# Copying the scan's products out of PSUM on ScalarE and masking them in SBUF on GpSimd

## The chip, the cores and the metric

The kernel runs on one core of a Trainium2 chip. Such a core has five engines with queues of their own: TensorE (PE in the profile, and PEld for its weight loads), VectorE (DVE), ScalarE (ACT), GpSimd (POOL) and SyncE (SP), which here only issues transfers. Matrix products land in PSUM; the other operands live in SBUF. GpSimd has no operation on PSUM in this kernel. An engine carries out its queue in order, and an instruction at the head of a queue that waits for another engine holds what is behind it.

The metric is the device time of one execution in microseconds (us), taken as the median of several runs.

## The reference, cut to what matters

One layer of an encoder: a half-step feed-forward network, a mixing layer, a second half-step feed-forward network, on 1024 tokens of 1024 features in float32. The mixing layer has eight attention heads and eight heads of a recurrent scan, which runs in both directions. The scan's step is

```python
def _rwkv7_step(state, inp):
    r, w, k, v, kk, kka = inp
    sa = jnp.einsum('dbhvk,dbhk->dbhv', state, kk)
    state = state * w[..., None, :] - sa[..., :, None] * kka[..., None, :] + v[..., :, None] * k[..., None, :]
    y = jnp.einsum('dbhvk,dbhk->dbhv', state, r)
    return state, y
```

`d` is the direction (2), `h` the head (8), and the state of each is 64 x 64. 1024 such steps follow one another.

## The kernel before, in words

The scan is not stepped token by token. The 1024 tokens are cut into 16 chunks of `C` = 64, and two chunks (`BLK` = 2) make a block, so there are eight blocks. Inside a chunk the steps are solved as a triangular system, from products of the chunk's own vectors; only the 64 x 64 state goes from chunk to chunk. Four methods do the work for a block `n`:

- `prep` (line 783) loads the inputs for both directions `d`, scales them by the running decay, and forms the products inside each chunk. For each chunk `i` it fills two PSUM banks, one for each parity `par` of the head (`lp`, line 830): four head pairs side by side, 128 rows by 128 columns each. The rows are two halves of 64 tokens: the half `half(par)` holds the products with the vector called `kka` in the reference, the other half those with `k`. The columns are two halves as well: 0 to 63 with `kk`, 64 to 127 with `r`. A token may only see earlier ones, so each 64 x 64 quadrant has to be triangular: without its diagonal for `kk`, with it for `r`. On line 832 VectorE multiplies each bank by a table of zeros and ones (`tri`) and writes it to the tile `lm` in SBUF. The three PSUM banks of tag `pp` are shared by `lp` and by the transposes `bp` (line 838), which ScalarE copies out on line 840. At the end (line 846) four transfers on SP's queue store the diagonal 32 x 32 blocks of the quadrant `kka` by `kk` in DRAM.
- `solve` (line 850) loads them again as `X`, and VectorE inverts all of them at once in 31 steps of two small operations each (lines 866 and 868) that wait for one another. GpSimd's queue then stores the inverse (lines 872 and 873).
- `merge` (line 875) loads the inverse over GpSimd's queue (lines 883 and 886) and joins the 32 x 32 inverses to 64 x 64 by products (lines 894 and 900). It reads the part of `lm` that lies above the diagonal blocks, in the same quadrant.
- `chain` (line 918) goes through the two chunks. On line 928 it first overwrites the quadrant `kka` by `kk` of `lm`, which is no longer needed, with other factors. For each chunk there are then the products `xu`, `st` and `y` (lines 937 to 952), ScalarE's copies between them (lines 944 and 954), VectorE's update of the state `sv` (line 968), and loads of values `uv` and `sv` on GpSimd's queue (line 908).

Blocks 0 and 1 are prepared among the last projections of the layer's input (lines 1269 and 1270). Then the loop over the blocks calls, for each `n`, `merge(n)`, `chain(n)`, and `upto(n + 3)`, which prepares and solves block `n + 3` (lines 1285 to 1299), so that up to three blocks are prepared ahead; `lm` has a buffer for each of them. Beside this, PE multiplies the attended values by their part of the output weights (`project_attended`, line 1066).

The framework's planner, which takes the order of the code as priority and goes by modelled costs, fixes the order of the instructions on each engine when the program is built, and places the waits between engines. A change to some instructions can therefore reorder their neighbours. Waits follow from the tiles' parts that are written and read.

The constants come in `mix_constants` (line 1146) and are made on the host in `_tables` (line 1394).

Of the kernel before, what the change touches and what calls it, by code (L numbers as in the profile page):

```python
# [13 lines left out]
OP = mybir.AluOpType  # L14
# [12 lines left out]
C, NC_, BLK = 64, 16, 2  # L27
# [4 lines left out]
def _ap(src, off, pat):  # L32
    return bass.AP(tensor=src.tensor, offset=src.offset + off, ap=pat)
# [130 lines left out]
class _Kernel:  # L164
# [618 lines left out]
    def prep(self, n, p, psum, big):  # L783

        nc, V, A, T = self.nc, self.nc.vector, self.nc.scalar, self.nc.tensor
        flat = lambda z: z.rearrange("p a t -> p (a t)")
        chunks = lambda z: z.rearrange("p a (i t) -> p a i t", i=BLK)
        ls = slice(n * TB, (n + 1) * TB)
        lm = big.tile([128, 2, 2, BLK, 4, 128], F32, name="lm", tag="lm")
        gc = big.tile([128, 2, 4, BLK], F32, name="gc", tag="gc")  # L790
        blk = dict(lm=lm, pr=[], bt=[], gc=gc)
        for d in range(2):
            b = n if d == 0 else NC_ // BLK - 1 - n
            ts = slice(b * TB, (b + 1) * TB)
            th = {}
            for nm in "wa":
                th[nm] = p.tile([128, 4, TB], F32, name="th_" + nm, tag="th_" + nm, bufs=2)
                self.load(th[nm], self.lr_d[nm][d][:, :, ls].rearrange("a p t -> p a t"))
            x3 = p.tile([128, 3, 4, TB], F32, name="in3", tag="in3", bufs=1)
            self.load(x3.rearrange("p j a t -> p (j a) t"), self.rk_d[:, :, ts].rearrange("a p t -> p a t"))  # L800
            x = {nm: x3[:, j, :, ::-1] if d else x3[:, j] for j, nm in enumerate(("r", "k", "kk"))}
            cum = th["w"]
            e1 = self.e1
            e4 = e1.rearrange("p (a i) t -> p a i t", i=BLK)
            A.activation(e4[:, :, :, 1:C + 1], chunks(cum), AF.Exp)
            A.activation(flat(cum), flat(cum), AF.Exp, scale=-1.0)
            ei = chunks(cum)
            V.tensor_copy(gc[:, d], e4[:, :, :, C])
            pt = big.tile([128, 4, BLK, 128], F32, name="pr", tag=f"pr{d}")
            V.tensor_tensor(pt[:, :, :, 0:C], chunks(x["kk"]), e4[:, :, :, 0:C], op=OP.mult)  # L810
            V.tensor_tensor(pt[:, :, :, C:], chunks(x["r"]), e4[:, :, :, 1:C + 1], op=OP.mult)
            bk = p.tile([128, 4, BLK, 192], F32, name="bk", tag="bk", bufs=2)
            bb = bk[:, :, :, 0:C]
            V.scalar_tensor_tensor(bb, chunks(th["a"]), 1.0, chunks(x["kk"]), op0=OP.add, op1=OP.mult)
            V.scalar_tensor_tensor(bb, bb, 0.5, ei, op0=OP.mult, op1=OP.mult)
            A.copy(bk[64:, :, :, 2 * C:], bk[64:, :, :, 0:C])
            kd = th["a"]
            for pr in range(4):
                A.activation(kd[:, pr, :], kd[:, pr, :], AF.Identity, scale=self.kah[:, pr:pr + 1],
                             bias=self.ka1[:, pr:pr + 1])  # L820
            V.tensor_tensor(kd, kd, x["k"], op=OP.mult)
            V.tensor_tensor(bk[:, :, :, C:2 * C], chunks(kd), ei, op=OP.mult)
            self.nc.sync.dma_start(self.kd_d[d][:, :, ls].rearrange("a p t -> p a t"), kd)
            bt = big.tile([128, BLK, 2, 4, 64], F32, name="bt", tag=f"bt{d}")
            both = [(slice(o, o + 64), o) for o in (0, 64)]
            for i in range(BLK):
                ps = [psum.tile([128, 4, 128], F32, name="lp", tag="pp") for par in range(2)]
                for pr in range(4):
                    for par, (hs, ko) in enumerate(both):
                        T.matmul(ps[par][:, pr, :], bk[hs, pr, i, ko:ko + 128], pt[hs, pr, i, :], start=True, stop=True)  # L830
                for par in range(2):
                    V.tensor_tensor(lm[:, par, d, i], ps[par], self.tri[:, None, :].to_broadcast([128, 4, 128]),
                                    op=OP.mult)
            pb = [psum.tile([128, BLK, 4, 64], F32, name="bp", tag="pp") for par in range(2)]
            for i in range(BLK):
                for pr in range(4):
                    for par, (hs, ko) in enumerate(both):
                        T.transpose(pb[par][:, i, pr, :], bk[hs, pr, i, ko:ko + 128], self.ident[hs, hs])
            for par in range(2):
                A.copy(bt[:, :, par], pb[par])  # L840
            for k, v in (("pr", pt), ("bt", bt)):
                blk[k].append(v)
        for par in range(2):
            for k in range(2):
                r0 = par * 64 + k * 32
                self.nc.sync.dma_start(_ap(self.x_d[n % 4], (k * 2 + par) * 16 * 1024, [[32, 32], [1024, 16], [1, 32]]),
                                  lm[r0:r0 + 32, par, :, :, :, k * 32:k * 32 + 32].rearrange("p d i a t -> p (d i a) t"))
        return blk
# [296 lines left out]

    def mix_constants(self, p):
        io = self.io
        for nm in ("ones2", "tri", "cen"):
            t = p.tile([128, 128], F32, name="k_" + nm)
            self.load(t, io["k_" + nm])  # L1150
            setattr(self, nm, t)
# [242 lines left out]
def _tables():  # L1394

    e = -np.arange(0, HD, 2, dtype=np.float32) / np.float32(HD)
    inv = np.power(10000.0, e.astype(np.float64)).astype(np.float32)
    ang = (np.arange(S, dtype=np.float32)[:, None] * inv[None, :]).astype(np.float64)
    c, s = np.cos(ang).astype(np.float32), np.sin(ang).astype(np.float32)
    i, j = np.arange(128)[:, None], np.arange(640)[None, :]  # L1400
    dist = np.abs(j - 256 - i)
    n = (dist <= 64).astype(np.int64) + ((dist <= 256) & (dist % 4 == 0))
    bias12 = np.where(n > 0, np.log(np.maximum(n, 1)), NEG).astype(np.float32)
    blk = np.arange(128) // 64
    same = blk[:, None] == blk[None, :]
    a = np.arange(64)
    lo, di = (a[:, None] < a[None, :]), (a[:, None] <= a[None, :])
    tri = np.tile(np.concatenate([lo, di], 1), (2, 1)).astype(np.float32)
    return {"k_rope": np.concatenate([c, c, -s, s], 1), "k_ones2": same.astype(np.float32), "k_tri": tri,
            "k_cen": (np.eye(128) - same / 64).astype(np.float32),  # L1410
            "k_bias12": bias12}

# [23 lines left out]
```

## Time and profile before

| | us |
|---|---|
| runs | 2351.04, 2352.01, 2360.32 |
| median | 2352.01 |
| profiled execution | 2359.91 |
| its span, first to last instruction | 2357.9 |
| mean granted TensorE clock | 0.956 |

The span is 2.0 us shorter than the profiled execution's time, and that execution lies near the slowest of the three runs. In the profile, "L832" is line 832 of the kernel. A group of instructions reads: line, engine, operation, output `<-` inputs by the program's names, shapes, count, then busy time in us and the mean duration in ns, then the engine's idle time just before them and what ended it. A row of the waits reads: who waited, for whom, total us, times, longest. In a timeline a row begins with its start and its duration in us. The scan's blocks are prepared from 1216 to 1503 us of the span, and its chunks run from 1312 to 1577 us; the feed-forward networks lie before and after, and take most of the span.

### The profile page before, as it was taken

Reading aid. Unit: us, or ns where it says so; the run is one execution under the profiler, and the core shown is the slowest. Engines: PE = TensorE matmul, PEld = TensorE weight load, DVE = VectorE, ACT = ScalarE, POOL = GpSimd, SP = SyncE. Lnnn points to the kernel's source line nnn. Section 1 sums busy time; section 2 is a strip of 40 time slices with the busy share of each in tenths; the row PEclk is TensorE's granted clock in tenths of the full one; section 3 lists DMA queues with packets and bytes.
Section 4 is the critical chain, followed back from the end, with each engine's and each line's share of the span. In section 5 each row is a group of like instructions: output and inputs, shape, how many; then the busy total and the mean of one; then the engine's idle time right before and its main releaser. Section 6 shows DMA issues by size and latency. Waiting matters only on the chain. (4 is left out here: it accounts for less than half of the span.)

```text
span 2357.9 us, 39484 instructions
## 1 busy us (share of the span) xinstructions
PE 2216.0 (94%) x14532; PEld 1788.8 (76%) x14532; DVE 1782.4 (76%) x2957; ACT 1035.0 (44%) x1958; POOL 609.7 (26%) x732
## 2 busy tenths in 40 slices
PE   6999999999999998999996899989699999999997
PEld 4788888878877676787775777766578888887886
DVE  8899999865676244766658778737899999986565
ACT  4332223354577412666554646445443323235453
POOL 6244444410000010111202242332334444441000
PEclk8999999999999998999997799989899999999999
DMA  5254544485662513323268877577434454547665
GB/s 157 98 171 154 177 143 170 166 262 193 207 217 85 200 45 120 99 79 81 68 167 201 212 187 197 140 233 250 156 108 168 167 174 143 174 156 258 193 191 180
DMA packets 359380, 386.04 MB, mean 164 GB/s; under 512 B 74258, under 2 KB 265618, under 8 KB 359188
## 3 DMA queue, kind: packets, MB, share of 16 engines
q1 hardware_dynamic: 308512, 276.43, 38.8%
q0 software_dynamic: 30320, 94.44, 11.2%
q10 hardware_dynamic: 20356, 12.66, 1.9%
q8 instruction: 114, 1.87, 0.3%
q14 instruction: 78, 0.64, 0.1%
HBM read 257.53 MB, written 125.89 MB: 163 GB/s over the span
## 5 line engine op out<-in xcount | busy, mean ns | idle before, releaser
L186 ACT ACTIVATE wh<-raw 128x512 fp32r<-128x512 f32 (+1 forms) x273 | 168.1, 626 | 267.4 <-PE gu L81 92.9
L81 PE MATMUL gu<-xh,wh 128*128 128x512 f32 x704 | 277.1, 394 | 1.1 <-ACT xh L186 1.1
L187 DVE TENSOR_TENSOR wl<-raw,wh 128x512 fp32r<-128x512 f32 (+1 forms) x273 | 273.8, 1006 | 4.4 <-ACT wh L186 3.2
L81 PE MATMUL gu<-xl,wh 128*128 128x512 f32 x704 | 276.1, 392 | 0.0
L81 PE MATMUL gu<-xh,wl 128*128 128x512 f32 x704 | 275.7, 392 | 0.0
L415 PE MATMUL pd<-gl,gwh 128*128 128x512 f32 x616 | 241.4, 392 | 3.0 <-DVE gl L187 3.0
L415 PE MATMUL pd<-gh,gwl 128*128 128x512 f32 x616 | 240.7, 391 | 0.0
L415 PE MATMUL pd<-gh,gwh 128*128 128x512 f32 x616 | 240.1, 391 | 0.4 <-DVE row L86 0.4
L86 DVE TENSOR_TENSOR row<-gu,row 128x512 f32<-128x512 f32 x308 | 206.4, 682 | 25.0 <-PE gu L81 24.6
L187 DVE TENSOR_TENSOR gwl<-graw,gwh 128x512 fp32r<-128x512 f32 (+1 forms) x176 | 116.9, 667 | 128.6 <-ACT gwh L186 126.5
L116 POOL DMA_DIRECT2D d_hid<-row x154 | 84.7, 551 | 473.3 <-DVE row L114 450.9
L186 ACT ACTIVATE gwh<-graw 128x512 fp32r<-128x512 f32 (+1 forms) x176 | 101.3, 576 | 189.9 <-PE pd L415 160.0
L81 PEld LDWEIGHTS gu<-xh,wh 128*128 128x128 f32 x704 | 133.4, 190 | 30.2 <-ACT xh L186 2.8
L81 PEld LDWEIGHTS gu<-xl,wh 128*128 128x128 f32 x704 | 133.3, 189 | 27.7
L81 PEld LDWEIGHTS gu<-xh,wl 128*128 128x128 f32 x704 | 133.1, 189 | 27.4
L415 PEld LDWEIGHTS pd<-gl,gwh 128*128 128x128 f32 x616 | 116.1, 188 | 28.2 <-DVE gl L187 4.3
L415 PEld LDWEIGHTS pd<-gh,gwh 128*128 128x128 f32 x616 | 115.8, 188 | 25.5 <-DVE row L86 0.7
L415 PEld LDWEIGHTS pd<-gh,gwl 128*128 128x128 f32 x616 | 116.2, 189 | 24.1
L187 DVE TENSOR_TENSOR gl<-raw,gh 128x512 fp32r<-128x512 f32 x160 | 113.0, 717 | 17.5 <-ACT gh L186 17.2
L94 ACT ACTIVATE row<-row 128x512 f32<-128x512 f32 x44 | 27.7, 633 | 222.5 <-DVE row L86 215.0
L145 POOL TENSOR_TENSOR ws<-ws 128x512 f32<-128x512 f32 x88 | 114.2, 1297 | 1.2
L186 ACT ACTIVATE gh<-raw 128x512 fp32r<-128x512 f32 x160 | 98.0, 621 | 34.9 <-DMA raw<-in_ffn_w_down_dram 21.7
(356 smaller groups left out, 5366.8 us busy)
## 6 DMA issues: line engine op xcount, KB each, us to landing
d_hid<-row POOLq DMA_DIRECT2D x154, 256.0 KB, 2.4
graw<-d_hid SPq DMA_DIRECT2D x132, 256.0 KB, 3.0
raw<-in_ffn_w_gate_dram SPq DMA_DIRECT2D x88, 256.0 KB, 3.0
raw<-in_ffn_w_up_dram SPq DMA_DIRECT2D x88, 256.0 KB, 3.4
ws<-in_ffn_w_down_dram SPq DMA_DIRECT2D x88, 256.0 KB, 4.6
d_ws<-ws POOLq DMA_DIRECT2D x88, 256.0 KB, 2.3
raw<-d_ws SPq DMA_DIRECT2D x88, 256.0 KB, 2.7
raw<-in_ffn_w_down_dram SPq DMA_DIRECT2D x66, 256.0 KB, 3.5
```

Source lines behind the costliest of these rows:

```text
L81: self.K.nc.tensor.matmul(ps, a[:, k, :], b[:, k, :], start=(k == 0 and i == 0), stop=(k == 3 and i == 2))
L86: add = lambda o, x: V.tensor_tensor(o, ps, x, op=OP.add)
L94: A.activation(y[:, 0], y[:, 0], AF.Silu)
L116: put = lambda n, y: G.dma_start(self.hid[n - 1, j // 2], y)
L145: G.tensor_tensor(o, a, b, op=OP.subtract)
L186: self.nc.scalar.activation(h, src, AF.Copy)
L187: (eng or self.nc.vector).tensor_tensor(l, src, h, op=OP.subtract)
L415: T.matmul(ps[x], a[:, ts], b, start=(m == 0 and k == 0), stop=(m == NM - 1 and k == 2))
```

## The change

The eight masked evictions per block on VectorE become eight plain copies on ScalarE. When both chunks of a direction are copied, GpSimd sets the elements that must be zero to zero in SBUF, in place: for each parity one select over the half of the rows that belongs to `k`, all 128 columns, both chunks and four head pairs (64 partitions x 1024 elements), and one over the other half of the rows, columns 64 to 127 only (64 partitions x 512 elements). The quadrant `kka` by `kk` is left unmasked: the solve reads only the strictly upper part of its diagonal blocks, the merge the block above them, and the chain overwrites it. The table `tri` is dropped, on the host and in the constants that are loaded.

```diff
--- before.py
+++ after.py
@@ -829,8 +829,14 @@
                     for par, (hs, ko) in enumerate(both):
                         T.matmul(ps[par][:, pr, :], bk[hs, pr, i, ko:ko + 128], pt[hs, pr, i, :], start=True, stop=True)
                 for par in range(2):
-                    V.tensor_tensor(lm[:, par, d, i], ps[par], self.tri[:, None, :].to_broadcast([128, 4, 128]),
-                                    op=OP.mult)
+                    A.copy(lm[:, par, d, i], ps[par])
+            for par, (hs, ko) in enumerate(both):
+                ks = both[1 - par][0]
+                nc.gpsimd.affine_select(out=lm[ks, par, d], in_=lm[ks, par, d], pattern=[[0, BLK * 4], [1, 2], [1, C]],
+                                        compare_op=OP.is_ge, fill=0.0, base=-1, channel_multiplier=-1)
+                nc.gpsimd.affine_select(out=lm[hs, par, d, :, :, C:], in_=lm[hs, par, d, :, :, C:],
+                                        pattern=[[0, BLK], [0, 4], [1, C]], compare_op=OP.is_ge, fill=0.0, base=0,
+                                        channel_multiplier=-1)
             pb = [psum.tile([128, BLK, 4, 64], F32, name="bp", tag="pp") for par in range(2)]
             for i in range(BLK):
                 for pr in range(4):
@@ -1145,7 +1151,7 @@
 
     def mix_constants(self, p):
         io = self.io
-        for nm in ("ones2", "tri", "cen"):
+        for nm in ("ones2", "cen"):
             t = p.tile([128, 128], F32, name="k_" + nm)
             self.load(t, io["k_" + nm])
             setattr(self, nm, t)
@@ -1403,10 +1409,7 @@
     bias12 = np.where(n > 0, np.log(np.maximum(n, 1)), NEG).astype(np.float32)
     blk = np.arange(128) // 64
     same = blk[:, None] == blk[None, :]
-    a = np.arange(64)
-    lo, di = (a[:, None] < a[None, :]), (a[:, None] <= a[None, :])
-    tri = np.tile(np.concatenate([lo, di], 1), (2, 1)).astype(np.float32)
-    return {"k_rope": np.concatenate([c, c, -s, s], 1), "k_ones2": same.astype(np.float32), "k_tri": tri,
+    return {"k_rope": np.concatenate([c, c, -s, s], 1), "k_ones2": same.astype(np.float32),
             "k_cen": (np.eye(128) - same / 64).astype(np.float32),
             "k_bias12": bias12}
```

## The prediction

> **What bounds the kernel now.** I read the page's busy times first, then a table of stretches around the scan, then who waits for whom in it, then the groups of VectorE (DVE) there. The page:
>
> ```profile
> span 2357.9 us, 39484 instructions
> PE 2216.0 (94%) x14532; PEld 1788.8 (76%) x14532; DVE 1782.4 (76%) x2957; ACT 1035.0 (44%) x1958; POOL 609.7 (26%) x732
> ```
>
> TensorE (PE) is busy in 94% of the span, VectorE in 76%; ScalarE (ACT) and GpSimd (POOL) have room. The page says nothing of the stage that the change touches, so here is the table of stretches (PE, PEld, DVE, ACT, POOL busy, granted clock, DMA share, GB/s):
>
> ```profile
> 1240.00:1280.00 40.00, 32.02 (x202) 25.34 (x202) 34.60 (x98) 18.61 (x37) 4.07 (x6) 0.87 0.74 191
> 1280.00:1300.00 20.00, 4.25 (x33) 3.41 (x31) 14.42 (x48) 9.62 (x16) 11.46 (x20) 0.50 1.03 226
> 1320.00:1510.00 190.00, 178.50 (x2897) 145.48 (x2898) 155.51 (x460) 101.05 (x189) 61.70 (x103) 0.93 0.71 184
> 1510.00:1580.00 70.00, 62.37 (x1305) 50.21 (x1304) 29.24 (x86) 31.95 (x60) 32.61 (x43) 0.90 0.70 198
> ```
>
> Two places differ. From 1320 to 1510 us, five blocks of the scan, PE works 178.5 of 190 us: 11.5 us are open at most. DVE works 155.5, and is the second engine to fill up. From 1280 to 1300 PE stands almost still, at half its clock: the first merge waits there for the first solve, which DVE does. So DVE matters before 1300, and after 1320 only where PE waits for it. Those waits (engine and line, what it waited for, us, times, longest), the first two inside 1320 to 1510, the third from the view of line 832 over the whole run, the fourth from 1200 to 1320:
>
> ```profile
> PE lp L830 <- DVE lm L832: 6.6, 6, 1.4
> DVE lm L832 <- PE lp L830: 3.2, 2, 2.8
> ...
>   PE lp L830: 7.7, 8
> ...
> PE pa L894 <- DMA d<-d_t: 8.2, 1, 8.2
> ```
>
> PE waits 7.7 us in all for the masked evictions of line 832 to free a PSUM bank. That is the only wait that the change removes from PE directly.
>
> **The change part by part.** What DVE does in 1320 to 1510 (groups; busy us, mean ns):
>
> ```profile
> L868 DVE TENSOR_TENSOR Ti<-Ti,ttmp 128x126 f32<-128x126 f32 (+22 forms) x157 | 39.6, 252 | 3.6
> L866 DVE TENSOR_TENSOR ttmp<-X,Ti 128x126 f32<-128x126 f32 (+22 forms) x157 | 39.3, 250 | 3.3
> L832 DVE TENSOR_TENSOR lm<-lp,k_tri 128x512 f32<-128x512 f32 x40 | 27.4, 684 | 3.3 <-PE lp L830 3.2
> L968 DVE TENSOR_TENSOR sv<-st,gc 64x512 f32<-64x512 f32 x20 | 13.8, 688 | 4.6 <-PE st L937 4.0
> ...
> L1078 DVE TENSOR_TENSOR yal<-yq,yah 128x512 fp32r<-128x512 f32 x6 | 4.1, 684 | 0.0
> L870 DVE COPY X<-Ti 128x512 f32<-128x512 f32 x6 | 3.6, 600 | 0.2
> ```
>
> *Removed from DVE.* Per block 8 masked evictions (2 directions, 2 chunks, 2 parities) of 684 ns: 5.5 us; 64 of them over the run, 43.8 us. In the five blocks that is 27.4 us, with 3.2 us of waiting in front: 30.6 us.
>
> *Added to ScalarE.* Eight plain copies per block from PSUM, 128x512. The same shape and direction stands in the trace:
>
> ```profile
> L840 ACT COPY bt<-bp 128x512 f32<-128x512 f32 x20 | 11.7, 586 | 22.2 <-PE bp L838 22.2
> PEld st L937 <- ACT uv L954: 3.7, 10, 0.7
> ```
>
> 8 x 0.586 = 4.7 us per block; ACT's load goes from 101.1 to 124.5 of 190 us, 66%. The idle 34% hides it. If that cover is gone at a given moment, what stands behind a copy that waits for PE are the chain's copies of lines 944 and 954, for which PE waits next; each can be late by one copy, 0.586 us. The least is nothing, the most 16 chunks x 2 x 0.586 = 19 us. The weight loads' wait for line 954, 3.7 us now, is the nearest row; scaled with the load (66 to 53%) it grows by about 1 us, which I take. In return a bank is freed in 586 ns instead of 684, by an engine with more idle time: of the 7.7 us that PE waits for line 832 I take 5 back (none to all 7.7).
>
> *Added to GpSimd.* Per block eight in-place selects on 64 partitions: four over 8 x 2 x 64 = 1024 elements and four over 2 x 4 x 64 = 512. The trace has one such operation, in the making of the identity; beside it the nearest operations with one or no input, and the subtraction with two:
>
> ```profile
> masks.py:199 POOL TENSOR_SCALAR_AFFINE_SELECT ident<-ident 128x128 f32<-128x128 f32 x1 | 0.3, 319 | 0.1
> L1143 POOL TENSOR_SCALAR w0h<-w0h 128x8 f32<-128x8 f32 x1 | 0.2, 232 | 4.5 <-DMA w0h<-in_rwkv_w_dram 4.5
> L1130 POOL TENSOR_TENSOR mu<-c_rwkv_mu_prev,c_rwkv_mu_next 128x15 f32<-128x15 f32 x1 | 0.2, 218 | 3.9 <-DMA c_rwkv_mu_next<-in_rwkv_mu_next_dram 3.9
> L202 POOL MEMSET one<- 1x128 f32 x1 | 0.2, 194 | 0.3 <-POOLq L1424 0.3
> L1424 POOL MEMSET const-float32-0.0<- 128x1 f32 x1 | 0.1, 98 | 0.2 <-issue 0.2
> L145 POOL TENSOR_TENSOR ws<-ws 128x512 f32<-128x512 f32 x88 | 114.2, 1297 | 1.2
> ```
>
> A start cost of 98 ns (the smallest memset) leaves 221 ns for 128 elements, 1.73 ns each: 1.87 and 0.98 us, 11.4 us per block. A start cost of 232 ns (the small one-input operation) leaves 0.68 ns: 0.93 and 0.58 us, 6.0 us per block. The 218 ns of the 15-element operation hold 15 elements at some 2 ns (the slope between it and the 1297 ns row), so 185 ns are start; that leaves 1.05 ns per element, 1.26 and 0.72 us, 7.9 us per block. I take 7.9, since that row is closest in kind, and keep 6.0 and 11.4. The Trainium skill, GPSIMD Engine Reference, section 3.1, gives about 1.8 cycles per element at 1.2 GHz (769 ns for 512 elements) for a tight loop; by it the selects would take an estimated 9.2 us per block, the DVE term below would be 10 us and the sum about +11, where the one row here gives +3.9.
>
> *What that does to VectorE.* POOL works in the feed-forward stage beside DVE, and there the rows show a price (DVE first, then POOL, from 95 us on):
>
> ```profile
> 96.31 2.54 DVE L187 TENSOR_TENSOR wl<-raw,wh 128x512 fp32r<-128x512 f32 x1
> 98.78 5.47 DVE L114 TENSOR_TENSOR row<-row 128x512 f32<-128x512 f32 x1
> ...
> 97.00 1.29 POOL L145 TENSOR_TENSOR ws<-ws 128x512 f32<-128x512 f32 x1
> 99.34 1.29 POOL L145 TENSOR_TENSOR ws<-ws 128x512 f32<-128x512 f32 x1
> 100.59 1.29 POOL L126 TENSOR_TENSOR row<-row 128x512 f32<-128x512 f32 x1
> 102.39 1.30 POOL L145 TENSOR_TENSOR ws<-ws 128x512 f32<-128x512 f32 x1
> ...
> L86 DVE TENSOR_TENSOR row<-gu,row x308: 673/681/693, 63.0 to 2130.4; 128x512 f32<-128x512 f32 x154
> ```
>
> A DVE operation with both inputs in SBUF lasts 5.47 us instead of 0.68 while POOL runs three subtractions, and ends when POOL has ended; line 86, with one input in PSUM, takes 673 to 693 ns in the same stage, always. POOL's own rows stay at 1.3. So DVE gives way, for the whole of POOL's time. The removed eviction read PSUM and was of the kind that isn't held up; of what stays on DVE in the scan (155.5 - 27.4 = 128.1 us), all but lines 968, 1078 and 870 (21.5 us) and one tiny copy reads SBUF twice, above all the 62 small steps of each solve. DVE will want to work in about 85% of the time of the selects (its 155.5 us and the gaps of some 60 ns between dependent small steps, of 190). Five blocks: 5 x 7.9 x 0.85 = 33.6 us of holding up against 30.6 us removed: +3 us. Bounds: 5 x 6.0 x 0.56 - 30.6 = -14 us (0.56 is (128.1 - 21.5)/190, without the gaps), and 5 x 11.4 - 30.6 = +26 us. Over the six blocks prepared beside the scan the middle value is +3.6 us, which I count in full, since PE and DVE are both close to full. The Trainium skill, SBUF — State Buffer, section "Who interferes with whom", says that whichever of the two starts first holds the shared port pair for that one instruction; the row above is harder, DVE being held over three POOL operations. By the rule DVE would get an operation in between two selects, the bursts below would cost an estimated 2 us and the sum be +1; by the row they cost 5.
>
> *The burst.* Twice per block, after the copies of a direction, four selects stand in a row (3.9 us). If line 968, the state for the next chunk, falls into one, PE stands still for it. 16 chunks, a chance of about 2 x 3.9/38 = 0.2 (38 us is a block's period, 190/5), 2 us each: 6 us; the planner orders some of it away, I take 5 (0 to 16 x 3.9 = 62 if it always hit).
>
> *Before 1300.* DVE, lines around the first solve:
>
> ```profile
> 1237.96 0.69 DVE L822 TENSOR_TENSOR bk<-th_a,th_w 128x512 f32<-128x512 f32 x1
> 1239.90 1.29 DVE L832 TENSOR_TENSOR lm<-lp,k_tri 128x512 f32<-128x512 f32 x2 [1.25 <-PE lp L830]
> 1242.04 1.29 DVE L832 TENSOR_TENSOR lm<-lp,k_tri 128x512 f32<-128x512 f32 x2 [0.85 <-PE lp L830]
> 1243.25 0.18 DVE L866 TENSOR_TENSOR ttmp<-X,Ti 128x31 f32<-128x31 f32 x1
> 1276.36 0.60 DVE L870 COPY X<-Ti 128x512 f32<-128x512 f32 x1
> 1235.63 1.11 SPq L182 DMA_DIRECT2D X<-d_x  x2
> ```
>
> Solve 0 starts at 1243.25 behind four evictions, though its input was sent for at 1235.6; it could start 1.29 + 1.29 + 2.1 = 4.7 us sooner, and four more evictions inside it give 2.7: 7.4 us. The eight selects of block 1 fall into it: 7.9 x 0.85 = 6.7. Net -0.7 us, between 6.0 x 0.56 - 7.4 = -4 and 11.4 - 7.4 = +4.
>
> *Queues.* The store of the diagonal blocks to DRAM (SP's queue) is issued behind the selects in the code, but reads only the quadrant that no select writes, so it waits for ACT's copies alone; were it held for the last two selects, the price is 2 us on X. The selects stand on POOL's queue between the loads of lines 883 to 908 and the stores of 872 and 873; each can be 3.9 us later. The masked parts are read three blocks of 38 us later, so the selects themselves can wait. The dropped load of the mask table is one of three small ones far ahead, and worth nothing; PE's work there hides it.
>
> **Sum.** -5 (banks) + 1 (ACT) + 3.6 (DVE) + 5 (bursts) - 0.7 (first solve) = +3.9 us. The profiled execution took 2359.9 us, 7.9 above the median 2352.0 of the three runs; carried over to the median: 2356 us. 0.5% is 11.8 us, about what a measurement of this kernel can tell from no change, so this counts as no change.
>
> **Rivals.**
> - *GpSimd sets VectorE's pace (slower).* Selects at 1.87 and 0.98 us, DVE always held. DVE gets 26 us more in five blocks; of its 34.5 us without work there the waits can give back about half, so 13 us show, 16 in six blocks; +4 at the first solve, +5 bursts, nothing gained at the banks: +25, 2377 us. It decides from about 9.5 us of selects per block on. For it: the 5.47 us row. Against it: only one row prices a select.
> - *VectorE's relief counts (faster).* Selects at 0.93 and 0.58 us, in gaps: -7.7 (banks), -4 (first solve), -3 (what else of PE's 11.5 open us hangs on DVE): -15, 2337 us. For it: the waits shown. Against it: PE is 94% full there.
> - *POOL's queue becomes the wait (slower).* A select that waits for a copy holds the chain's loads behind it; these stand up to 19.9 us at the queue's head today, for buffers:
>
> ```profile
> POOL sv L908 <- DVE Ti L868: 19.9, 1, 19.9
> ```
>  so they are early, and lose 3.9 us without harm; if two merges were late by a burst each and the chain with them: +14 with the sum, 2366 us.
>
> **How the numbers follow.** Forecast 0.45; VectorE's pace 0.30; relief 0.20; POOL's queue 0.05. Faster by over 0.5% needs under 2340 us: 0.20. Slower needs over 2364: 0.35. The same: 0.45. The range, 2336 to 2380, reaches a little past both rivals; the forecast's own is 2342 to 2364.
>
> **What would show it.** Right: no DVE row on line 832, an ACT copy of 0.59 us x64; selects near 1.3 and 0.7 us; the means of lines 866 and 868 up from 250 ns, with single ones of 1 to 4 us beside selects; PE in the scan near 94%. Wrong: selects over 2 us (then slower), or lines 866 and 868 unchanged beside selects (then the holding up isn't there, and the time is towards 2337); the first merge earlier by more than 4 us; or PE waiting for ACT's copies in line 830 as long as for DVE before.

## The result and the profile after

| | before | after |
|---|---|---|
| median of the runs, us | 2352.2 | 2387.52 |
| runs | 2351.04 to 2360.32 | 2386.26 to 2390.62 |
| profiled execution, us | 2359.91 | 2387.97 |
| its span, us | 2357.9 | 2386.2 |

The changed kernel is slower: its time is 1.0145 times that of before, with a 95% interval of 1.0120 to 1.0171. That is 34 us of 2352 (28 to 40). It lies outside the predicted range, and on the side that had a chance of 0.35. Below, a time "over before" is always that ratio less one, times 2352 us. The plain medians of the same runs differ from it by up to 7 us (e6 below: 26 in place of 33), so a few us between two runs say nothing.

The page of the changed kernel gives the span and each engine's busy time. Lines behind 832 are shifted by six: the solve's two operations are lines 872 and 874, the merge's loads 889 and 892, the chain's loads of values 914, the chain's first product 947.

```profile
span 2386.2 us, 39574 instructions
...
PE 2209.0 (93%) x14532; PEld 1784.2 (75%) x14532; DVE 1779.8 (75%) x2893; ACT 1063.3 (45%) x2022; POOL 671.2 (28%) x796
```

VectorE is busy for 1779.8 us and was for 1782.4. It does 64 operations less, and the 43.8 us that they took are back in its busy time: something else on it has become longer. The table of stretches has the same columns as the one in the prediction (PE, PEld, DVE, ACT, POOL busy, granted clock, DMA share, GB/s).

```profile
1280.00:1300.00 20.00, 8.63 (x64) 6.91 (x64) 14.81 (x33) 8.60 (x17) 11.74 (x18) 0.67 0.86 210
1320.00:1510.00 190.00, 152.82 (x2616) 125.62 (x2616) 133.70 (x360) 109.65 (x211) 90.62 (x134) 0.89 0.68 173
```

From 1320 to 1510 us PE works 152.8 us where it worked 178.5, on 2616 matrix instructions in place of 2897, at a granted clock of 0.89 in place of 0.93. The loss is there and ahead of it, where the chain starts. The view of the tile `lm` gives line, engine, operation, count, shortest/median/longest in ns, and the first and last start; its two indented rows say who waited for `lm` (us, times).

```profile
L947 PE MATMUL xu<-sv,lm x512: 221/222/370, 1331.3 to 1602.6; 128*64 128x64 f32 x160, 64*64 64x64 f32 x11
...
L832 ACT COPY lm<-lp x64: 564/588/609, 1221.2 to 1530.7; 128x512 f32<-128x512 f32 x64
L835 POOL TENSOR_SCALAR_AFFINE_SELECT lm<-lm x32: 1152/1161/1692, 1222.9 to 1532.0; 64x1024 f32<-64x1024 f32 x32
L837 POOL TENSOR_SCALAR_AFFINE_SELECT lm<-lm x32: 651/658/1644, 1224.6 to 1533.2; 64x512 f32<-64x512 f32 x32
...
  POOL lm L835: 107.4, 16
...
  PE lp L830: 2.1, 3
```

The copies last 588 ns, the selects 1161 and 658 ns. PE waits 2.1 us for a bank where it waited 7.7. The first product of the chain starts at 1331.3 us, and did at 1312.2. New is the first indented row: GpSimd's queue stands 107.4 us with a select at its head that waits for ScalarE's copies. This is what that looks like at the first merge, in the timeline of GpSimd (start, duration, operation, and in brackets the idle time before it and what ended it):

```profile
1292.43 1.16 POOL L835 TENSOR_SCALAR_AFFINE_SELECT lm<-lm 64x1024 f32<-64x1024 f32 x1 [6.63 <-ACT lm L832]
...
1297.96 0.68 POOL L889 DMA_DIRECT2D d<-d_t  x1
...
1314.11 1.48 POOL L835 TENSOR_SCALAR_AFFINE_SELECT lm<-lm 64x1024 f32<-64x1024 f32 x1 [12.26 <-ACT lm L832]
...
1318.09 0.63 POOL L914 DMA_DIRECT2D uv<-d_vt  x1
...
1325.16 2.46 POOL L914 DMA_DIRECT2D sv<-d_vt  x4
```

The merge's loads (line 889) and the chain's first loads (line 914) stand behind selects of block 2, which wait 6.63 and 12.26 us for that block's copies. What PE itself waits for there, from 1296 to 1343 us, is this:

```profile
PE lp L830 <- DVE bk L822: 13.4, 1, 13.4
PE po L1070 <- DVE yal L1084: 6.1, 1, 6.1
PE xu L947 <- DMA sv<-d_vt: 3.4, 2, 2.8
```

PE's queue stands 13.4 us with products of block 2 that wait for VectorE's line 822. The first merge's products stand behind them and begin as soon as these have begun (1307.5 and 1308.3 us), so it is not its late loads that the merge waits for last, as it was before (8.2 us). Only the chain's first products wait for loads, 3.4 us for `sv`.

And on VectorE, in the same run, the solve's steps beside four selects, first VectorE's timeline, then GpSimd's:

```profile
1250.76 0.22 DVE L874 TENSOR_TENSOR Ti<-Ti,ttmp 128x58 f32<-128x58 f32 x1
1251.01 1.05 DVE L872 TENSOR_TENSOR ttmp<-X,Ti 128x56 f32<-128x56 f32 x1
1252.09 0.68 DVE L874 TENSOR_TENSOR Ti<-Ti,ttmp 128x56 f32<-128x56 f32 x1
1252.80 1.11 DVE L872 TENSOR_TENSOR ttmp<-X,Ti 128x81 f32<-128x81 f32 x1
1253.95 0.67 DVE L874 TENSOR_TENSOR Ti<-Ti,ttmp 128x81 f32<-128x81 f32 x1
1254.65 0.24 DVE L872 TENSOR_TENSOR ttmp<-X,Ti 128x78 f32<-128x78 f32 x1
```

```profile
1250.77 1.23 POOL L835 TENSOR_SCALAR_AFFINE_SELECT lm<-lm 64x1024 f32<-64x1024 f32 x1 [8.59 <-ACT lm L832]
1252.05 0.65 POOL L837 TENSOR_SCALAR_AFFINE_SELECT lm<-lm 64x512 f32<-64x512 f32 x1
1252.66 1.15 POOL L835 TENSOR_SCALAR_AFFINE_SELECT lm<-lm 64x1024 f32<-64x1024 f32 x1
1253.87 0.66 POOL L837 TENSOR_SCALAR_AFFINE_SELECT lm<-lm 64x512 f32<-64x512 f32 x1
```

A step of 0.22 us takes as long as the select beside it, and one step gets in between two selects. So the trace offers two causes at once, and a third and fourth cannot be excluded by looking: ScalarE's copies may be in the way of other copies, and the planner has written a new order for every engine. I call them:

- **T1**: the selects stand on GpSimd's queue ahead of the merge's and the chain's loads, and wait there for the copies.
- **T2**: the selects hold VectorE up, whose solve the next merge waits for.
- **T3**: ScalarE's copies delay the chain's copies behind them.
- **T4**: the planner's new order costs time by itself.

### The profile page after: what moved, and what is told of

Its sections match the earlier page's. It is cut to its first block, busy times and chain, and to the rows that moved or that the text cites. A ratio compares the mean times of both kernels' runs of the same rounds, so it can differ in the third digit from the quotient of the medians.

```text
span 2386.2 us, 39574 instructions
## 1 busy us (share of the span) xinstructions
PE 2209.0 (93%) x14532; PEld 1784.2 (75%) x14532; DVE 1779.8 (75%) x2893; ACT 1063.3 (45%) x2022; POOL 671.2 (28%) x796
```

## The experiments

The results first; the edits and expectations follow. "First chain" is the start of the first product of the chain, "five blocks" the time from the first copy of `y` of chunk 0 to that of chunk 10, both from the timelines of each run (before: 1323.5 to 1517.9 us, 194.4). The last column tells whether selects run while the chain runs.

| run | over before, us (95%) | first chain | five blocks | selects beside the chain |
|---|---|---|---|---|
| before | 0 | 1312.2 | 194.4 | no |
| after | 34.1 (28 to 40) | 1331.3 | 206.7 | yes |
| e1 copies only | 1.9 (-2 to 6) | 1310.0 | 196.0 | no |
| e2 memsets for selects | 18.6 (13 to 25) | 1319.0 | 194.9 | no |
| e4 selects one block late | 20.5 (14 to 27) | 1312.0 | 205.0 | yes |
| e5a selects from block 3 | 17.6 (11 to 24) | 1311.6 | 210.1 | yes |
| e5b selects to block 2 | 22.1 (16 to 28) | 1327.3 | 197.3 | no |
| e6 selects beside the mask | 32.7 (24 to 41) | 1316.0 | 214.5 | yes |
| e7 selects behind merge's loads | 24.9 (19 to 31) | 1304.6 | 212.5 | yes |
| e8 the wait alone | 4.7 (1 to 9) | 1315.7 | 196.1 | no |
| e9 memsets behind merge's loads | -0.9 (-4 to 3) | 1303.3 | 199.0 | no |
| e10 selects for block 0 only | 11.8 (8 to 16) | 1318.4 | 206.9 | no |
| e11 mask, and selects late | 35.5 (31 to 40) | 1306.0 | 222.5 | yes |
| e13 two blocks | 18.6 (14 to 23) | 1311.0 | 213.6 | few |
| e14 block 0, memsets | 13.9 (9 to 19) | 1316.9 | 204.2 | no |
| e15 block 0, copies only | 10.6 (6 to 15) | 1315.3 | 204.1 | no |

**e1, the copies without the selects.**

```diff
-                    A.copy(lm[:, par, d, i], ps[par])
+                    A.activation(lm[:, par, d, i], ps[par], AF.Copy, scale=0.001)
...
-                nc.gpsimd.affine_select(out=lm[ks, par, d], in_=lm[ks, par, d], pattern=[[0, BLK * 4], [1, 2], [1, C]],
...
-                nc.gpsimd.affine_select(out=lm[hs, par, d, :, :, C:], in_=lm[hs, par, d, :, :, C:],
...
```

> ScalarE copies the products out of PSUM and nothing masks them (a scale of 0.001 in the copy keeps the numbers finite; the masking is left out, and the products come out 1000 times too small). No instruction of GpSimd is added. If the selects on GpSimd's queue (T1) or their hold on VectorE (T2) make the 35 us, this run is as fast as before or a little faster, 2335 to 2352 us, with the first chain at 1305 to 1312 us. If ScalarE's copies, queued ahead of the chain's copies, make it (T3), it is slower by 12 to 35 us: 2364 to 2387. If the planner's new order by itself does (T4), likewise 2364 or more.

It is as fast as before: ratio 1.0008, interval 0.9991 to 1.0025. T3 falls as the cause of the loss: with 64 copies on ScalarE there is none. Two of its rows are worth a look, the stretch of five blocks and PE's largest wait around it (1330 to 1530 us):

```profile
1320.00:1510.00 190.00, 165.69 (x2923) 137.07 (x2923) 135.46 (x414) 119.46 (x230) 60.11 (x98) 0.95 0.72 180
```

```profile
PE po L1063 <- ACT yao L1082: 16.6, 5, 4.4
```

VectorE is rid of 20 us of work (135.5 in place of 155.5), and the blocks are no faster: even with masking for free, this kernel only equals the one before. Its order is another than that of before, so what the run gives is the sum of the relief, the copies and the order; what the relief is worth in the old order is not shown. And the changed kernel's list of waits also has PE waiting 16.1 us for that same copy of ScalarE; here the same wait stands without a loss.

**e6, the selects without the copies.**

```diff
-                    A.copy(lm[:, par, d, i], ps[par])
+                    V.tensor_tensor(lm[:, par, d, i], ps[par], self.tri[:, None, :].to_broadcast([128, 4, 128]),
+                                    op=OP.mult)
```

> VectorE masks out of PSUM as before, and GpSimd's selects run as well, on what is already masked. T1: the selects wait at the head of GpSimd's queue for VectorE's evictions in place of ScalarE's copies, and hold the loads of the merge and of the chain: 25 to 40 us slower than before, 2377 to 2392. T2: VectorE has the evictions and the holding up too, so slower still: 2390 to 2420. T3 (ScalarE's copies are to blame): within 10 us of before.

33 us over before (24 to 41): the selects alone make as much loss as the whole change. By its number it speaks for T1, and against a T2 that comes on top of VectorE's evictions; the pairs below set that right.

**e2, memsets in the selects' places.**

```diff
-                nc.gpsimd.affine_select(out=lm[ks, par, d], in_=lm[ks, par, d], pattern=[[0, BLK * 4], [1, 2], [1, C]],
...
-                nc.gpsimd.affine_select(out=lm[hs, par, d, :, :, C:], in_=lm[hs, par, d, :, :, C:],
...
+                nc.gpsimd.memset(lm[ks, par, d], 0.0)
+                nc.gpsimd.memset(lm[hs, par, d, :, :, C:], 0.0)
```

> ScalarE's copies as in the changed kernel; the selects are replaced by memsets over the same regions, which stand at the same places of GpSimd's queue and wait for the same copies, but read nothing and are shorter (all products but the unmasked quadrant are zeros: the masked products are left out of the result). T1: the wait for the copies remains, so most of the loss remains: 2370 to 2387. T2 (the selects hold VectorE up): the loss goes, 2340 to 2358, and the means of the solve's steps in 1320 to 1540 fall back from 300 to 250 ns.

The built program has the same instructions in the same order on every engine as the changed kernel, a memset for each select, so T4 is the same in both. The groups of GpSimd from 1200 to 1600 us in e2, and of VectorE from 1320 to 1510, first e2, then the changed kernel:

```profile
L835 POOL MEMSET lm<- 64x1024 f32 x32 | 30.4, 950 | 98.5 <-ACT lm L832 98.5
```

```profile
L871 DVE TENSOR_TENSOR Ti<-Ti,ttmp 128x126 f32<-128x126 f32 (+22 forms) x151 | 38.6, 256 | 4.3
```

```profile
L874 DVE TENSOR_TENSOR Ti<-Ti,ttmp 128x126 f32<-128x126 f32 (+22 forms) x131 | 37.7, 288 | 3.8
```

The wait at the head of the queue is as long as ever, 98.5 us, and the memsets are nearly as long as the selects, 950 ns for 1161. But the solve's steps are back from 288 to 256 ns, and five blocks take 194.9 us as before. The time lies between the two expectations: the loss falls from 34 to 19 us. Some 15 us (7 to 24, from the intervals of both) are thus VectorE's hold-up (T2); the other 19 us lie in the place on the queue, the copies and the order together. The two traces say where: with memsets the first chain starts 12 us earlier, five blocks take 12 us less, and the last copy of `y` ends at 1586.3 us in place of 1609.6 (before: 1578.2).

**e4, the selects one block late.** The new method `mask` holds the eight selects of a block.

```diff
+                if n:
+                    self.mask(blk[n - 1]["lm"])
                 blk[n] = self.prep(n, sp, pp, (R0, R1)[n])
```

> The same copies and the same selects, but the selects of a block are issued at the start of the next block's preparation, when its copies are long done. T1: GpSimd's head waits for ScalarE fall from 107 us to under 20, the first merge's loads go out at 1287 to 1293 us as before, and the time comes within 12 us of before: 2345 to 2364. T2: the selects still hold VectorE up for as long, so the loss remains at 2375 to 2390. T4: any new order costs some 20 us: 2370 or more.

The edit did not do what it was to do: the planner moved the selects forward again, and the wait for ScalarE's copies stayed at 93.1 us (107.4 in the changed kernel). Still the first chain starts as early as before, at 1312.0. So the loss does not lie ahead of the chain; in the scan five blocks take 205.0 us, 11 more than before.

**e7 and e9, out of the queue's way.** In e7 an explicit order puts the selects behind `ld`, the last load of the merge, when their copies are two blocks old.

```diff
+        if n:
+            with self.tc.issue_after(ld.ins):
+                self.mask(lm)
         pa = psum.tile([128, NI, 32], F32, name="pa", tag="mg")
```

> The changed kernel, but from block 1 on the selects of a block stand on GpSimd's queue right behind the loads of that block's merge, when their copies are two blocks old; the number and sizes of the selects are the same. T1 (the queue waits): GpSimd waits for ScalarE's copies under 20 us in all, the merge's first loads stand at 1278 to 1291 us, and the time is 2350 to 2362. T2 (the selects hold VectorE up wherever they stand): the means of the solve's two steps stay near 290 to 310 ns and the time is 2368 or more.

In e9, `mask` holds memsets:

```diff
-                nc.gpsimd.affine_select(out=lm[ks, par, d], in_=lm[ks, par, d], pattern=[[0, BLK * 4], [1, 2], [1, C]],
...
+                nc.gpsimd.memset(lm[ks, par, d], 0.0)
+                nc.gpsimd.memset(lm[hs, par, d, :, :, C:], 0.0)
```

> The kernel with the selects behind the merge's loads, the selects replaced by memsets of the same regions (950 and 519 ns in the earlier run with memsets; all products but the unmasked quadrant are zeros). GpSimd's queue is occupied almost as long and waits for as little; only the reading is gone. If the 25 us there come from VectorE being held up by the selects (T2), the loss goes: 2348 to 2360, with the solve's steps at 250 to 260 ns in place of 325. If they come from occupying the queue, or from the order that the planner then finds, it stays at 2368 or more.

These two again have the same instructions in the same order on every engine. In e7 the wait for the copies falls to 13.9 us in all and the first chain starts 8 us earlier than before; it is 25 us slower nonetheless. In e9 the loss is gone: ratio 0.9996, interval 0.9981 to 1.0011. VectorE's groups from 1320 to 1510 us, of e7 and then of e9:

```profile
L880 DVE TENSOR_TENSOR ttmp<-X,Ti 128x126 f32<-128x126 f32 (+22 forms) x141 | 46.3, 328 | 5.8 <-DMA X<-d_x 1.7 <-issue 0.4
L882 DVE TENSOR_TENSOR Ti<-Ti,ttmp 128x56 f32<-128x56 f32 (+22 forms) x142 | 45.8, 323 | 4.2
```

```profile
L877 DVE TENSOR_TENSOR ttmp<-X,Ti 128x126 f32<-128x126 f32 (+22 forms) x151 | 38.9, 257 | 7.4 <-DMA X<-d_x 1.7 <-POOL Ti L873 1.7
L879 DVE TENSOR_TENSOR Ti<-Ti,ttmp 128x126 f32<-128x126 f32 (+22 forms) x151 | 38.6, 256 | 4.5
```

The same place in both runs, first e7 (VectorE, then GpSimd), then e9 (VectorE, then GpSimd):

```profile
1365.15 0.69 DVE L985 TENSOR_TENSOR sv<-st,gc 64x512 f32<-64x512 f32 x1
1365.88 1.08 DVE L882 TENSOR_TENSOR Ti<-Ti,ttmp 128x78 f32<-128x78 f32 x1
1367.20 0.94 DVE L1089 TENSOR_TENSOR yat<-yat,rs 128x512 f32<-128x512 f32 x1 [0.24 <-DMA yat<-d_ya]
1368.06 1.21 DVE L880 TENSOR_TENSOR ttmp<-X,Ti 128x100 f32<-128x100 f32 x1
1369.30 0.68 DVE L882 TENSOR_TENSOR Ti<-Ti,ttmp 128x100 f32<-128x100 f32 x1
```

```profile
1365.72 1.15 POOL L858 TENSOR_SCALAR_AFFINE_SELECT lm<-lm 64x1024 f32<-64x1024 f32 x1
1366.94 0.66 POOL L860 TENSOR_SCALAR_AFFINE_SELECT lm<-lm 64x512 f32<-64x512 f32 x1
1367.55 1.61 POOL L858 TENSOR_SCALAR_AFFINE_SELECT lm<-lm 64x1024 f32<-64x1024 f32 x1
```

```profile
1361.73 0.26 DVE L877 TENSOR_TENSOR ttmp<-X,Ti 128x100 f32<-128x100 f32 x1
1362.02 0.26 DVE L879 TENSOR_TENSOR Ti<-Ti,ttmp 128x100 f32<-128x100 f32 x1
```

```profile
1361.56 0.95 POOL L858 MEMSET lm<- 64x1024 f32 x1
```

The step over 128x100 takes 1.21 and 0.68 us beside selects, and 0.26 us beside memsets. The 26 us between the two kernels (24.9 less -0.9, 19 to 33 from both intervals) are T2, measured with the same order. What else differs is the length, 0.95 us for 1.15, and that memsets leave zeros where the products were. The granted clock from 1320 to 1510 us is 0.96 in e9 and 0.91 in e7. It is 0.95 in e14 below, where the products of block 0 alone are zero, so the zeros are not needed for it; that they have a small part in the 26 us is not excluded.

**e8, the wait alone.** VectorE masks as before; in the selects' places stand memsets of 64x8 elements that are zero already.

```diff
                     V.tensor_tensor(lm[:, par, d, i], ps[par], self.tri[:, None, :].to_broadcast([128, 4, 128]),
                                     op=OP.mult)
+            for par in range(2):
+                nc.gpsimd.memset(lm[both[1 - par][0], par, d, :, :, 0:1], 0.0)
```

> The kernel before, with VectorE's masked evictions, and in the place of the selects one memset per direction and parity over 64x8 elements that are zero already: about 0.1 us each, but it stands at the same place of GpSimd's queue and waits for the same evictions. T1: the wait alone costs most of the first two thirds: 10 to 20 us over before, 2362 to 2372, with 80 us or more of waiting for VectorE at the queue's head. T2: nothing, 2348 to 2357.

Apart from these memsets the order on every engine is that of before. The view of `lm`:

```profile
L835 POOL MEMSET lm<- x32: 104/106/136, 1220.7 to 1505.0; 64x8 f32 x32
...
  POOL lm L835: 119.1, 28
```

119.1 us of waiting at the head of GpSimd's queue, more than in the changed kernel, and 5 us are lost (1 to 9), half of the least that T1 named. A wait's total says little of its price. But the run does not price T1 in the changed kernel: in the order of before, other loads stand behind the waits. The first merge's loads go out at 1287.6 us (before 1286.9, changed 1298.0), the chain's first loads of `sv` at 1294.0 (before 1292.6, changed 1325.2). What it shows is that waits with no urgent load behind them cost little.

**e5a and e5b, by blocks.** This is e5a; e5b has `n < 3` in both places.

```diff
-                    A.copy(lm[:, par, d, i], ps[par])
...
+                    if n > 2:
+                        A.copy(lm[:, par, d, i], ps[par])
+                    else:
+                        V.tensor_tensor(lm[:, par, d, i], ps[par], self.tri[:, None, :].to_broadcast([128, 4, 128]),
+                                        op=OP.mult)
+            if n > 2:
+                for par, (hs, ko) in enumerate(both):
...
```

> Blocks 0 to 2 are evicted and masked by VectorE as before, blocks 3 to 7 by ScalarE's copies and GpSimd's selects. T1: the 19 us lost ahead of the first chain come back (first chain at 1310 to 1316 us) and the loss in the scan stays: 12 to 20 us over before, 2364 to 2372. T2 alone would leave five eighths of 35 us, 22: 2374.

> The reverse: ScalarE's copies and GpSimd's selects for blocks 0 to 2, VectorE's masked evictions from block 3 on. T1: the first chain is late as in the changed kernel (1325 to 1332 us), and the scan then runs as before: 15 to 22 us over before, 2367 to 2374. T2 alone would leave three eighths, 13: 2365.

Both came out within or at the edge of what T1 had named, 17.6 and 22.1 us, and the places are right: with selects from block 3 on, the first chain is on time (1311.6) and the scan slow (210.1); with selects up to block 2 it is the reverse (1327.3 and 197.3). But the slow scan, which I had put down to the queue, is at least in large part VectorE's, as e7 and e9 show; in e5a too the solve's steps from 1320 to 1510 us last 308 ns in the mean.

**e11, the hold-up in the kernel before.** VectorE masks as before, no copy moves to ScalarE, and redundant selects run behind the merge's loads from block 1 on. Against the kernel before:

```diff
+        if n:
+            with self.tc.issue_after(ld.ins):
+                self.mask(lm)
         pa = psum.tile([128, NI, 32], F32, name="pa", tag="mg")
```

> The kernel before, with VectorE's masked evictions and without any copy of ScalarE; from block 1 on the eight selects of a block run as well, on what is masked already, behind the loads of that block's merge, where nothing has to be waited for. T2: the hold-up alone costs 7 blocks of 2.5 to 3.5 us: 17 to 25 us over before, 2370 to 2378, with the first chain at 1312 us as before. If the hold-up is hidden where VectorE is not the bound: under 8 us.

It is the slowest of all, 36 us over before, though no select waits for anything; the expectation had 17 to 25. The selects take 8.0 us per block, as in e7, but VectorE has the evictions too, and five blocks take 222.5 us. Its order also differs from that of before, and T4's part in it is not known.

**e10, e13, e14 and e15, in search of a faster version, and of T4.** e10 is e5a with `n == 0` in both places. e13 is e7 with copies for blocks 0 and 1 alone, and block 1's selects behind its merge's loads:

```diff
-                    A.copy(lm[:, par, d, i], ps[par])
+                    if n < 2:
+                        A.copy(lm[:, par, d, i], ps[par])
+                    else:
+                        V.tensor_tensor(lm[:, par, d, i], ps[par], self.tri[:, None, :].to_broadcast([128, 4, 128]),
+                                        op=OP.mult)
...
-        if n:
+        if n == 1:
             with self.tc.issue_after(ld.ins):
```

> ScalarE's copies and GpSimd's selects for block 0 alone, where VectorE's evictions stand ahead of the first solve and no load waits on GpSimd's queue; VectorE masks blocks 1 to 7 as before. If the first solve gains its 4.7 us and the rest stays: 2346 to 2351. If not, 2350 to 2358.

> ScalarE's copies for blocks 0 and 1, the selects of block 1 behind its merge's loads, VectorE's masked evictions from block 2 on. With all selects placed so, the first chain stood at 1305 us, 7 us ahead of before; if the scan then runs as before, 2344 to 2352; if the 7.3 us of selects in block 1 take it back, 2350 to 2360.

Both missed: 12 and 19 us over before. In e10 no select runs beside the chain, and yet five blocks take 206.9 us. So I took the selects out of e10, once for memsets as in e2 (e14), once for nothing (e15, below), with the same order of all other instructions on every engine.

```diff
                     if n == 0:
-                        A.copy(lm[:, par, d, i], ps[par])
+                        A.activation(lm[:, par, d, i], ps[par], AF.Copy, scale=0.001)
...
-            if n == 0:
-                for par, (hs, ko) in enumerate(both):
...
```

> As with ScalarE's copies and GpSimd's selects for block 0 alone, but memsets in place of the selects (the masked products of block 0 are left out). The order of the instructions is the same on every engine. If the planner's order is what cost 13 us there: 2366 to 2376 again. If the selects' hold on VectorE ahead of the first solve: 2350 to 2358.

> As with ScalarE's copies for block 0 alone, without selects or memsets (block 0's products are copied with a scale of 0.001 and stay unmasked; the masking of block 0 is left out). The order of the other instructions is the same on every engine. Planner's order: 2366 to 2376 again. GpSimd's queue or the selects: 2350 to 2358.

```profile
1320.00:1510.00 190.00, 171.27 (x2798) 140.75 (x2798) 152.17 (x440) 98.91 (x187) 61.83 (x103) 0.93 0.72 184
```

e15's stretch of five blocks: seven of the eight blocks work as before, the eighth differs by eight copies that are over when the scan begins, and the loss is still 10.6 us (6 to 15); with memsets it is 13.9 (9 to 19). An order that the planner found after a small edit costs that much here (T4). Which of its moves does it, I did not find out: no single wait of PE stands out in this run. No version beat the kernel before; e1 and e9, each in an order of its own, equal it.

**What is settled, and what is not.** Of the 34 us, 15 to 26 are VectorE held up by selects that read SBUF: 15 (7 to 24) by the pair after and e2, 26 (19 to 33) by the pair e7 and e9, each pair with one order. The traces agree: the solve's steps beside selects last 24 us longer in all in the changed kernel, and 23 in e7, and over the whole span VectorE is busy 31 us longer with selects than with memsets in both pairs (1779.8 and 1748.4, 1778.8 and 1747.8). What is left over, 8 to 19 us, is the place on the queue, the copies and the planner's order together. Of this, the trace of the changed kernel shows 3.4 us of PE waiting for the chain's first loads, and an order alone cost 11 us in another kernel; how the rest is shared stays open, since an edit that moves a select also moves the order.

## The prediction, point by point

- *Removed from DVE, 30.6 us in five blocks.* The evictions are gone as said, and VectorE's load fell from 155.5 to 135.5 us in e1. **This is the step that failed: "33.6 us of holding up against 30.6 us removed: +3 us".** It set off one against the other, as if VectorE's time were one sum. In two kernels without selects and with orders of their own nothing of the relief shows (e1: 1.9 us, -2 to 6; e9: -0.9, -4 to 3). The hold-up falls on the solve, 62 steps that wait for one another, and counts almost in full. This step alone would not have left the range: with 23 us of hold-up (the 19.5 below, over six blocks) in place of 3.6, the sum is +24, 2376 us. Beyond 2380 it is the 8 to 19 us of order and place on the queue, for which the sum had nothing.
- *The size of the hold-up.* It was too large. In e7 it is 141 x (328 - 257) + 142 x (323 - 256) ns = 19.5 us on the solve's steps in 1320 to 1510, where I had 33.6. I had taken a row of the feed-forward stage in which one operation of VectorE lasted over three of GpSimd. GpSimd's queue issues transfers between those three (at 98.24, 98.79, 101.82 and 103.63 us), which my lines left out; why the one operation was held over all of it stays open. Here one step gets in after each select. The Trainium skill, SBUF — State Buffer, "Who interferes with whom", says that the engine that issues first has the shared ports for its whole instruction; the trace of e7 agrees (1.21 us, then 0.68, beside a select each). The same section says that GpSimd instructions which only write do not hold such an operation up: so it is, 0.26 us beside memsets. The gaps between dependent steps, which I had at some 60 ns, are 34 ns in the kernel before; the share of 0.85 would have been 0.87.
- *GpSimd's selects, 1.26 and 0.72 us.* Right in size: 1.16 and 0.66 by the medians, 7.3 us per block, and 7.9 with the selects that were themselves held up.
- *ScalarE's copies, 0.586 us, +1.* Right: 0.588, and 1.9 us over before (-2 to 6) for all of them in e1, with the relief and the order in it.
- *Banks, -5.* PE's wait fell from 7.7 to 2.1 us, 5.6 us as said. None of it shows in the time of e1.
- *Before 1300, -0.7.* The first solve ends at 1279.4 in place of 1276.4 us: 3 us late, inside the bounds of -4 to +4. Without selects (e1) it ends at 1269.6, 6.8 us sooner where I had 7.4, and the first chain still starts only 2 us sooner: in the order of e1, as in that of the changed kernel, PE's queue stands with products of block 2 that wait for VectorE (13.6 us), and the merge behind them.
- *The burst, +5.* Line 968 (974 after) keeps its mean of 687 ns in 1320 to 1510; it reads PSUM. In the changed kernel none of them starts inside a select; e7 has one from 1531.21 us, inside a select that runs from 1531.03 to 1532.20, and it takes 0.69 us. So a burst does not hold it. What is late is the solve.
- *Queues.* "Each can be 3.9 us later" counted a select's duration and forgot what it waits for: 6.63 and 12.26 us ahead of the first merge's and the first chain's loads. PE's wait for such loads is 3.4 us there. What the place on the queue costs by itself in this order was not measured; e2, which has the waits, the copies and the order without the reading, loses 18.6 us, and the rival on POOL's queue had +14 with the rest.
- *The rivals.* "GpSimd sets VectorE's pace" named the right engine, but asked for selects of 9.5 us per block to decide, because of the same setting off; it came with 7.3 to 7.9. "VectorE's relief counts" did not come: its condition was selects of 0.93 and 0.58 us, and e1, with no select at all, is no faster than before. That the planner's order may cost 10 us had no place in the prediction.

## What to carry to other kernels

Before work is moved off an engine, ask whether anything waits for that work, and set no relief of an engine off against a delay of the one chain on it that the next stage waits for. Small operations on VectorE with both inputs in SBUF, in a chain, are a bad neighbour for GpSimd work that reads SBUF, while work that only writes does them no harm. Where a planner orders the program, compare kernels whose orders are the same: two such pairs priced the hold-up here, which the runs with an order of their own had left mixed.

## What was not expected of the hardware

- Of the 496 solve steps in the changed kernel's trace, the 46 that overlap a select last 771 ns in the mean, the others 254. In e2 the 85 that overlap a memset in a select's place last 248.
- The hold works both ways. In e7 a select that begins while VectorE is inside an operation with two SBUF inputs (line 1089, from 1367.20) lasts 1.61 us in place of 1.15; the longest in the changed kernel has 1.69.
- A select costs (1161 - 658)/512 = 0.98 ns per element and 155 ns more, a memset of the same regions (950 - 519)/512 = 0.84 and 88.
